# Output blocks 2 and 3 computed ahead at the end of the attention, with the partial sums of blocks 0 and 1 parked in DRAM

## The chip, the cores and the metric

The kernel runs on one core of a Trainium2 chip. The metric is the device time of one execution in microseconds. Engines are named as the profile names them: PE is TensorE, DVE is VectorE, ACT is ScalarE, POOL is GpSimd, SP is SyncE, whose queue here issues most of the DMA transfers. PSUM is the memory that matmuls add into; the kernel uses it in banks of 128 x 512 float32.

## What is computed

Two layers of a decoder on 1024 tokens of width 1024: a retention layer, then a differential attention with 16 heads. The change lies where the second layer's attention ends and its output projection begins. Cut to that part, the reference is:

```python
def diff_attn_mixer(h, w_in, w_out, ...):
    proj = h @ w_in                       # q, k, v and the gate g
    ...                                   # two softmaxes a head, their difference times v
    out = lax.map(block, (qb, starts))    # (heads, tokens, 128)
    out = rmsnorm(out, subln_g, eps=GN_EPS) * (1.0 - lambda_init)
    y = out.transpose(0, 2, 1, 3).reshape(B, S, D_INNER)
    gated = jax.nn.silu(g.astype(jnp.float32)) * y
    return gated.astype(w_out.dtype) @ w_out

x = x + rmsnorm(y, post_norm_g[i])
```

The product `gated @ w_out` is 1024 x 2048 times 2048 x 1024.

## The kernel before

**Numbers.** A float32 factor is split into a rounded high part and the rest (`gh`/`gl` or `wh`/`wl`), and a product takes three matmuls: high by high, high by low, low by high. ACT casts the high part, DVE or POOL subtracts it to get the low one.

**Tiles of the output projection.** The tokens are 8 blocks of 128, the output columns two halves of 512, the inner dimension 16 tiles of 128, one for each head. One block and half fills one PSUM bank and takes 16 x 3 matmuls of 128 x 512. `out_mm` issues them for a run of tiles; `gated8` loads eight tiles of gated attention from DRAM and splits them, in three buffers for each part.

**The attention** (`attention_layer`) runs heads and row blocks in the order `ORDER`, a step being one row block of a head: scores, softmax, transposes of the probabilities (`attn_t`), and after two row blocks the product with the values and a sum of squares. The softmax is on DVE and ACT, so PE would wait for it. Between these steps the kernel therefore pulls matmuls from `filler_gen`: the projections of later heads, and at last the output projection of token blocks 0 and 1, as far as it can go, that is inner tiles 0 to 11 of the first half. A clock of estimated PE time decides how many are pulled at each place; `late` is what of the filler is left for the last steps. The banks that these two blocks fill (`heads`) stay in use until the block is finished.

**Why it can go no further.** The gated tiles need a scale for each token and head, which `row_scales` makes in three batches of heads: 0 to 7, 8 to 11, 12 to 15. The last batch exists only when the attention has ended.

**The output stage** (`output_stage(1, ...)`) starts there. It runs blocks 2 to 7 in pairs over inner tiles 0 to 11, each in a bank of its own, and loads the weights of the second half of the columns meanwhile (`second_half`, two 512 KB loads a call). Then it finishes blocks 0 to 7 with the last quarter, inner tiles 12 to 15 (`product(..., 3)`, 12 matmuls a block). For that `gated` loads the raw values of the last four heads (`graw`, three buffers), the gate (`sgl`, one buffer) and the scales (`rsb`, two), multiplies by the gate on DVE and by the scales on POOL, stores the result for the second half, and splits it into `gh` and `gl`. `first` takes the squares and the scaled copy of a finished bank. The second half of the columns follows, block by block, from values stored in DRAM.

**What sets the order.** PE's instructions stand as the code calls them. On DVE, ACT, POOL and SP a scheduler chooses the order when the program is built, and each engine then works strictly in that order. A tile's buffer is given out again when the tile before it has been used for the last time.

Of the kernel before, what the change touches and what calls it, by code (L numbers as in the profile page):

```python
# [10 lines left out]
F32 = mybir.dt.float32  # L11
# [8 lines left out]
P = 128  # L20
# [3 lines left out]
TB = T // P  # L24
# [3 lines left out]
DH = 16  # L28
NE = 16
# [8 lines left out]
GOB = 1  # L38
ORDER = (6, 2, 3, 7, 4, 0, 1, 5)
LATE = 12  # L40
RATE = 40.4
BATCHES = ((0, 8), (8, 12), (12, 16))
LAMBDA_INIT = 0.8 - 0.6 * math.exp(-0.3)
# [7 lines left out]
class _Trunk:  # L51
# [59 lines left out]
        nc.vector.tensor_sub(gl, raw, _f32(gh))  # L111
        return gh, gl

    def out_mm(self, ps, g, slots, kt0, n, g0=0):
        nc = self.nc
        gh, gl = g
        for k in range(n):
            kt = kt0 + k
            w = slice((kt % 2) * 512, (kt % 2) * 512 + 512)
            wh, wl = (x[:, w] for x in slots[kt // 2])  # L120
            k += g0
            nc.tensor.matmul(ps, gh[:, k, :], wh, start=(kt == 0), stop=False)  # L122
            nc.tensor.matmul(ps, gh[:, k, :], wl, start=False, stop=False)  # L123
            nc.tensor.matmul(ps, gl[:, k, :], wh, start=False, stop=(kt == NE - 1))  # L124
            yield 0.65

    def norm_rows(self, pool, xt, gbc):
# [322 lines left out]
    def output_stage(self, layer, slots, nextR, prologue, head):  # L450
        nc, io = self.nc, self.io
        with ExitStack() as es:
# [4 lines left out]
            fp = self.pool(es, "fsb")  # L457
# [20 lines left out]
            def product(ps, hf, tb, kq):  # L478
                if WIDE[layer][hf] > kq:
                    if kq % 2 == 0:  # L480
                        for _ in self.out_mm(ps, self.gated8(layer, ((tb, kq * 4, 8),)), slots[hf], kq * 4, 8):
                            pass
                    return
                for _ in self.out_mm(ps, gated(tb, kq, hf), slots[hf], kq * 4, 4):
                    pass
# [6 lines left out]
            def second_half(t0):  # L492
                for t in (t0, t0 + 1):
                    self.load_out(layer, slots, 1, t, fp.tile([P, D], F32, tag="x", name="w_raw", bufs=2))

            def first(tb, ps):
                if not acc:
                    acc["y"] = fp.tile([P, TB, 512], F32, name="yacc")
                    acc["ss"] = fp.tile([P, TB, 2], F32, name="ssq")
                    acc["postg"] = fp.tile([P, D], F32, name="postg")  # L500
                    nc.sync.dma_start(acc["postg"], io["post_g"][layer:layer + 1, :].broadcast_to([P, D]))
                    if layer == 0:
                        acc["preg"] = fp.tile([P, D], F32, name="preg")
                        nc.sync.dma_start(acc["preg"], io["pre_g"][1:2, :].broadcast_to([P, D]))
                junk = fp.tile([P, D], F32, tag="x", name="junk", bufs=2)
                nc.scalar.activation(junk[:, 0:512], ps, AF.Square, accum_out=acc["ss"][:, tb, 0:1])
                nc.vector.tensor_mul(acc["y"][:, tb, :], ps, acc["postg"][:, 0:512])
                if layer == 0 and tb % 2 == 0:
                    second_half(tb)

            if layer == 0:
                lead = 2
                g = [self.gated8(0, ((tb, 8, 8),)) for tb in range(lead)]
                for tb in range(lead):
                    for _ in self.out_mm(head[tb], g[tb], slots[0], 8, 8):
                        pass
                    first(tb, head[tb])
            else:
                for t in range(6, 8):
                    self.load_out(1, slots, 0, t)  # L520
                for tb in range(2, TB, 2):
                    two = (tb, tb + 1)
                    g = [self.gated8(1, ((t, 0, 8),)) for t in two]
                    head += [bank() for t in two]
                    for t in two:
                        for _ in self.out_mm(head[t], g[t - tb], slots[0], 0, 8):
                            pass
                    g8 = self.gated8(1, tuple((t, 8, 4) for t in two))
                    for t in two:
                        for _ in self.out_mm(head[t], g8, slots[0], 8, 4, 4 * (t - tb)):  # L530
                            pass
                    second_half(tb - 2)
                second_half(TB - 2)
                for tb in range(TB):
                    product(head[tb], 0, tb, 3)
                    first(tb, head[tb])
                lead = TB
            for tb in range(lead, TB):
                ps = bank()
# [5 lines left out]
            for tb in range(TB):  # L545
# [3 lines left out]
                ps = bank()  # L549
# [25 lines left out]
    def attention_layer(self, HR, QR, pmm, ws0, slots):  # L575
        nc, io = self.nc, self.io
        with ExitStack() as es:
# [8 lines left out]
            wk = self.pool(es, "l1w")  # L586
# [31 lines left out]
            early = []  # L618
            heads = []

            def g_proj(h):
# [4 lines left out]
                for hf in range(2):  # L626
# [6 lines left out]
                    if h >= LATE:  # L633
                        nc.sync.dma_start(self.sgd[4 * hf:4 * hf + 4, :, h - LATE, :].rearrange("t p q -> p t q"), sg.rearrange("p (t q) -> p t q", t=4))
                    out.append(sg)
# [31 lines left out]
            def filler_gen():  # L667
                for h in range(1, DH):
                    yield from qk_proj(h)
                    if h % 2 == 0:  # L670
                        yield from v_proj(h // 2)
                    if h < LATE:
                        yield from g_proj(h)
                for h in range(LATE, DH):
                    yield from g_proj(h)
                for t in range(4, 6):
                    self.load_out(1, slots, 0, t)
                g = self.gated8(1, ((0, 8, 4), (1, 8, 4)))
                for tb in range(2):
                    ps = pmm.tile([P, 512], F32, tag="mm", name="ps_mm", bufs=2)  # L680
                    heads.append(ps)
                    yield from self.out_mm(ps, early[tb], slots[0], 0, 8)
                for tb in range(2):
                    yield from self.out_mm(heads[tb], g, slots[0], 8, 4, 4 * tb)

            filler = filler_gen()
            clk = {"pe": 0.0, "fill": 0.0}
# [177 lines left out]

            seq = [(h, i) for h in range(DH) for i in ORDER]
            total = 15 * 20.8 + 7 * 20.8 + (LATE - 1) * 10.4
            late = (DH - LATE) * 10.4 + 15.6
            load_bias(0)
            for _ in self.l1_qk(HR, QR, pmm, 0, ((0, 1), (1, 1)), ws0):  # L870
                pass
# [12 lines left out]
            for s, (h, i) in enumerate(seq):  # L884
                nxt = seq[s + 1] if s + 1 < len(seq) else None
# [60 lines left out]
    def run(self):  # L946
        nc, ctx = self.nc, self.ctx
# [14 lines left out]
        self.g0 = self.dr.tile([TB, P, NE, P], F32, name="g0")  # L962
        self.g1r = [self.dr.tile([TB, P, h1 - h0, P], F32, name="g1r%d" % h0) for h0, h1 in BATCHES]
        self.g1f = [self.dr.tile([TB, P, 8, P], F32, name="g1f%d" % k) for k in range(2)]
        self.x1d = self.dr.tile([T, D], F32, name="x1d")
        self.sgd = self.dr.tile([TB, P, DH - LATE, P], F32, name="sgd")
        self.ssd = [self.dr.tile([TB, h1 - h0, P], F32, name="ssd%d" % h0) for h0, h1 in BATCHES]
# [6 lines left out]
        pmm = self.pool(ctx, "pmm", PSUM)  # L974
# [16 lines left out]
        with ExitStack() as manual:  # L991
# [7 lines left out]
            early = [a(i) for i in (0, 1, 2, 3, 4, 12, 13, 14)] + [b(i) for i in range(8)]  # L999
# [3 lines left out]
            heads = self.attention_layer(RB, RA, pmm, ws0, pairs)  # L1003
# [78 lines left out]
```

## Time and profile before

| | us |
|---|---|
| median of 3 runs | 2182.5 (2181.49 to 2183.46) |
| the profiled execution, its own time | 2179.38 |
| its span | 2177.6 |
| PE busy in the span | 2132.8 (98%) |
| DVE, ACT, POOL busy | 1283.4, 851.6, 429.3 |

The span is what the trace covers, from the first instruction to the last. The attention of the second layer ends at about 2003 us, the last quarter of the first half runs from about 2055 to 2079, and the second half of the columns takes the rest. "Busy" of PE counts matmuls whose ends are modelled and which overlap, so the pace of PE is read from their starts. A row of a timeline gives start, duration, engine, line and operation, and in brackets how long the engine stood idle before it and what ended that.

### The profile page before, as it was taken

What the parts mean: (1) busy time and instruction counts of PE and PEld (TensorE: products, weight loads), DVE (VectorE), ACT (ScalarE), POOL (GpSimd) and SP (SyncE); (2) the same over time, 40 slices, a digit from 0 to 9 for tenths busy, and PEclk for the clock granted to TensorE, in tenths of its full rate; (3) what the DMA queues carried; (4) which work ended last, traced back from release to release, by engine and by line L of the source; (5) the groups of instructions that cost most, each with busy time, mean ns of one, the idle gap of its engine ahead of it and who ended that gap; (6) DMA issues with size and microseconds to landing.
All of it is one profiled execution on the core that took longest, in us unless ns stands there. A gap on an engine that the chain in (4) does not pass through costs nothing.

```text
span 2177.6 us, 31046 instructions
## 1 busy us (share of the span) xinstructions
PE 2132.8 (98%) x11861; PEld 1790.8 (82%) x11861; DVE 1283.4 (59%) x3155; ACT 851.6 (39%) x1638; POOL 429.3 (20%) x246
## 2 busy tenths in 40 slices
PE   8999999999999999999999999999999999999998
PEld 7888988898897888787888888888787878877776
DVE  6254344334437438646777666767766777776644
ACT  4121221122123333335455555554545555554321
POOL 2332501511512000121111111111133111211300
PEclk9999999999999999999999999999999999999999
DMA  4112112111213545311111111111244113334743
GB/s 167 62 39 68 57 39 73 47 54 54 64 57 99 179 155 174 113 48 42 49 37 42 49 40 42 39 38 43 84 135 136 47 38 95 112 104 146 257 150 134
DMA packets 98916, 185.48 MB, mean 85 GB/s; under 512 B 8848, under 2 KB 51024, under 8 KB 98640
## 3 DMA queue, kind: packets, MB, share of 16 engines
q1 hardware_dynamic: 63824, 166.50, 23.6%
q10 hardware_dynamic: 34944, 17.01, 2.6%
q8 instruction: 93, 1.52, 0.3%
q14 instruction: 55, 0.45, 0.1%
HBM read 147.67 MB, written 38.95 MB: 86 GB/s over the span
## 4 chain that ended last, share of the span: by engine, by line
PE 92%; DVE 3%; issue 1%; ACT 1%; DMA 1%; POOL 0%; ACTq 0%; DVEq 0%; POOLq 0%
PE ps_mm L158 6%; PE ps_mm L157 6%; PE ps_mm L159 5%; PE ps_mm L215 5%; PE ps_mm L122 5%; PE ps_mm L124 5%; PE ps_mm L123 5%; PE ps_mm L217 5%; PE ps_mm L216 5%; PE ps_t L809 3%; PE ps_ret L396 3%; PE ps_s L752 3%; PE ps_mm L650 3%; PE ps_mm L651 3%; PE ps_mm L652 3%; PE ps_mm L167 3%
## 5 line engine op out<-in xcount | busy, mean ns | idle before, releaser
L83 POOL TENSOR_TENSOR w_l<-w_raw,w_h 128x1024 fp32r<-128x1024 f32 x112 | 271.2, 2427 | 1168.8 <-ACT w_h L82 1165.3
L785 ACT ACTIVATE e<-ps_s,nm 128x896 f32<-128x896 f32 (+7 forms) x256 | 189.8, 742 | 103.4 <-DVE nm L783 93.8
L215 PE MATMUL ps_mm<-RB,w_h 128*128 128x512 f32 x512 | 209.4, 409 | 0.4 <-ACT RB L150 0.4
L157 PE MATMUL ps_mm<-RA,w_h 128*128 128x512 f32 x512 | 203.9, 398 | 1.2 <-DVE sg L426 1.1
L158 PE MATMUL ps_mm<-RA,w_h 128*128 128x512 f32 x512 | 204.6, 400 | 0.0
L216 PE MATMUL ps_mm<-RB,w_h 128*128 128x512 f32 x512 | 201.9, 394 | 1.0 <-DVE RB L151 1.0
L217 PE MATMUL ps_mm<-RB,w_l 128*128 128x512 f32 x512 | 202.5, 395 | 0.0
L159 PE MATMUL ps_mm<-RA,w_l 128*128 128x512 f32 x512 | 201.9, 395 | 0.0
L812 ACT CAST ath<-ps_t 128x512 fp32r<-128x512 f32 (+1 forms) x192 | 91.9, 479 | 227.0 <-PE ps_t L809 217.5
L780 DVE TENSOR_REDUCE mx<-ps_s 128x1 f32<-128x640 f32 (+2 forms) x192 | 119.5, 622 | 78.7 <-PE ps_s L755 74.4
L82 ACT CAST w_h<-w_raw 128x1024 fp32r<-128x1024 f32 x112 | 117.6, 1050 | 123.2 <-PE ps_mm L158 39.0
L650 PE MATMUL ps_mm<-w_h,RB 128*128 128x256 f32 x512 | 147.4, 288 | 0.0
L169 PE MATMUL ps_mm<-w_h,RA 128*128 128x256 f32 x512 | 146.1, 286 | 0.0
L167 PE MATMUL ps_mm<-w_h,RA 128*128 128x256 f32 x512 | 145.3, 285 | 0.5 <-ACT RA L150 0.5
L168 PE MATMUL ps_mm<-w_l,RA 128*128 128x256 f32 x512 | 145.2, 285 | 0.1
L111 DVE TENSOR_TENSOR g_l<-w_raw,g_h 128x1024 fp32r<-128x1024 f32 x60 | 82.7, 1378 | 105.7 <-ACT g_h L110 105.6
L651 PE MATMUL ps_mm<-w_l,RB 128*128 128x256 f32 x512 | 143.6, 280 | 0.0
L652 PE MATMUL ps_mm<-w_h,RB 128*128 128x256 f32 x512 | 143.6, 280 | 0.0
L110 ACT CAST g_h<-w_raw 128x1024 fp32r<-128x1024 f32 x60 | 63.0, 1051 | 172.2 <-PE ps_mm L123 126.4
L157 PEld LDWEIGHTS ps_mm<-RA,w_h 128*128 128x128 f32 x512 | 96.1, 188 | 24.5 <-DVE sg L426 1.6
L217 PEld LDWEIGHTS ps_mm<-RB,w_l 128*128 128x128 f32 x512 | 96.1, 188 | 23.7
L159 PEld LDWEIGHTS ps_mm<-RA,w_l 128*128 128x128 f32 x512 | 96.2, 188 | 22.3
(211 smaller groups left out, 5392.7 us busy)
## 6 DMA issues: line engine op xcount, KB each, us to landing
w_raw<-in_wn SPq DMA_DIRECT2D x64, 512.0 KB
w_raw<-in_wv SPq DMA_DIRECT2D x32, 512.0 KB
w_raw<-in_wo SPq DMA_DIRECT2D x32, 512.0 KB
w_raw<-g SPq DMA_DIRECT2D x32, 512.0 KB
w_raw<-g1f SPq DMA_DIRECT2D x24, 512.0 KB
xt<-in_x SPq DMA_DIRECT2D x16, 512.0 KB
w_raw<-in_wg SPq DMA_DIRECT2D x16, 512.0 KB
g<-go ACTq DMA_DIRECT2D x32, 256.0 KB
```

The source lines that it names most:

```text
L83: nc.gpsimd.tensor_sub(l, raw, _f32(h))
L157: nc.tensor.matmul(ps, wh[:, k], region[:, kt, cols], start=(kt == 0), stop=False)
L158: nc.tensor.matmul(ps, wh[:, k], region[:, 8 + kt, cols], start=False, stop=False)
L159: nc.tensor.matmul(ps, wl[:, k], region[:, kt, cols], start=False, stop=(kt == KT - 1))
L167: nc.tensor.matmul(ps, region[:, kt, cols], wh[:, k], start=(kt == 0), stop=False)
L215: nc.tensor.matmul(ps, wh[:, k], HR[:, kt, tok], start=(kt == 0), stop=False)
L216: nc.tensor.matmul(ps, wh[:, k], HR[:, 8 + kt, tok], start=False, stop=False)
L217: nc.tensor.matmul(ps, wl[:, k], HR[:, kt, tok], start=False, stop=(kt == KT - 1))
L650: nc.tensor.matmul(ps[:, t, :], HR[:, kt, cols], wh[:, k], start=(kt == 0), stop=False)
L651: nc.tensor.matmul(ps[:, t, :], HR[:, kt, cols], wl[:, k], start=False, stop=False)
L652: nc.tensor.matmul(ps[:, t, :], HR[:, 8 + kt, cols], wh[:, k], start=False, stop=(kt == KT - 1))
L785: nc.scalar.activation(e[:, 0:n], S[:, 0:n], AF.Exp, bias=nm, accum_out=(s0 if m == 0 else s1))
```

## The change

Blocks 2 and 3 join the filler. `AHEAD_TB = 4` says how many blocks go ahead. When blocks 0 and 1 have run inner tiles 0 to 11, ACT copies their banks to SBUF and stores them to a DRAM tensor `part`; the two banks then take blocks 2 and 3, which stay in them as blocks 0 and 1 did before. In the output stage blocks 4 to 7 run ahead of the last quarter, where 2 to 7 did. Blocks 0 and 1 then take a fresh bank for the last quarter, which starts a sum of its own, and `first` adds the parked partial sum on DVE. The tile into which it is loaded has the tag `graw`, that of the raw values of the last four heads. `late` rises from 41.6 + 15.6 to 41.6 + 31.2.

```diff
@@ out_mm
-    def out_mm(self, ps, g, slots, kt0, n, g0=0):
+    def out_mm(self, ps, g, slots, kt0, n, g0=0, k_first=0, k_last=NE - 1):
...
-            nc.tensor.matmul(ps, gh[:, k, :], wh, start=(kt == 0), stop=False)
+            nc.tensor.matmul(ps, gh[:, k, :], wh, start=(kt == k_first), stop=False)
             nc.tensor.matmul(ps, gh[:, k, :], wl, start=False, stop=False)
-            nc.tensor.matmul(ps, gl[:, k, :], wh, start=False, stop=(kt == NE - 1))
+            nc.tensor.matmul(ps, gl[:, k, :], wh, start=False, stop=(kt == k_last))
@@ output_stage
-            def first(tb, ps):
+            def first(tb, ps, part=None):
...
+                if part is not None:
+                    nc.vector.tensor_add(part, ps, part)
+                    ps = part
                 junk = fp.tile([P, D], F32, tag="x", name="junk", bufs=2)
...
-                for tb in range(2, TB, 2):
+                for tb in range(AHEAD_TB, TB, 2):
...
-                    second_half(tb - 2)
-                second_half(TB - 2)
+                    second_half(tb - AHEAD_TB)
+                for t in range(TB - AHEAD_TB, TB, 2):
+                    second_half(t)
                 for tb in range(TB):
-                    product(head[tb], 0, tb, 3)
-                    first(tb, head[tb])
+                    if tb < AHEAD_TB - 2:
+                        part = fp.tile([P, 512], F32, tag="graw", name="part", bufs=3)
+                        nc.sync.dma_start(part, self.part[tb])
+                        ps = bank()
+                        for _ in self.out_mm(ps, gated(tb, 3, 0), slots[0], 12, 4, k_first=12):
+                            pass
+                        first(tb, ps, part)
+                    else:
+                        ps = head[tb - AHEAD_TB + 2]
+                        product(ps, 0, tb, 3)
+                        first(tb, ps)
@@ filler_gen
-                for tb in range(2):
-                    ps = pmm.tile([P, 512], F32, tag="mm", name="ps_mm", bufs=2)
-                    heads.append(ps)
-                    yield from self.out_mm(ps, early[tb], slots[0], 0, 8)
-                for tb in range(2):
-                    yield from self.out_mm(heads[tb], g, slots[0], 8, 4, 4 * tb)
+                for t0 in range(0, AHEAD_TB, 2):
+                    last = 11 if t0 + 2 < AHEAD_TB else NE - 1
+                    pss, nxt = [], []
+                    for t in range(2):
+                        pss.append(pmm.tile([P, 512], F32, tag="mm", name="ps_mm", bufs=2))
+                        yield from self.out_mm(pss[t], early[t0 + t], slots[0], 0, 8, k_last=last)
+                        if last == 11:
+                            early.append(self.gated8(1, ((t0 + 2 + t, 0, 8),)))
+                    for t in range(2):
+                        yield from self.out_mm(pss[t], g, slots[0], 8, 4, 4 * t, k_last=last)
+                        if last == 11:
+                            part = wk.tile([P, 512], F32, tag="sg", name="part", bufs=3)
+                            nc.scalar.copy(part, pss[t])
+                            nc.scalar.dma_start(self.part[t0 + t], part)
+                        else:
+                            heads.append(pss[t])
+                    if last == 11:
+                        g = self.gated8(1, ((t0 + 2, 8, 4), (t0 + 3, 8, 4)))
...
-            late = (DH - LATE) * 10.4 + 15.6
+            late = (DH - LATE) * 10.4 + 7.8 * AHEAD_TB
```

How the order moves, at three places. Line numbers of the change are one to some thirty higher for the same statement. First PE at the seam between attention and output stage; `ps_o` holds the last values and, from L845, their sums of squares, and L857 transposes the sums for the last scales. Before:

```order
L824 MATMUL ps_o<-atl,RA 128x128
L825 MATMUL ps_o<-ath,RA 128x128
L845 MATMUL ps_o<-sqh,ones 128x256
L846 MATMUL ps_o<-sql,ones 128x256
L857 MATMUL ps_t<-ident,s0all 32x128
L122 MATMUL ps_mm<-RA,g_h 128x512
```

The same place in the change, where these rows follow a first triple of the same kind, which stands behind the last value product:

```order
L123 MATMUL ps_mm<-RB,g_h 128x512
L124 MATMUL ps_mm<-RB,g_h 128x512
L125 MATMUL ps_mm<-RB,g_l 128x512
L871 MATMUL ps_o<-sqh,ones 128x256
L872 MATMUL ps_o<-sql,ones 128x256
L883 MATMUL ps_t<-ident,s0all 32x128
```

Six output matmuls stand between the last values and their sum of squares, where none stood. In the same way 9 more stand ahead of the scores of the last head's row block 3 (12 for 3), 21 for 15 between the scores and the transposes of its row block 0, and 9 for none ahead of the last value product. In all 144 output matmuls stand before L883, and 72 before L857.

Second, SP's queue behind the seam. `graw_19808`, `graw_19840` and `graw_19868` are the raw values of blocks 0, 1 and 2 before; `graw_19818`, `graw_19854` and `graw_19883` those of the change. Before:

```order
L462 DMA graw_19808<-g1r12_82 128x512
L464 DMA sgl_19810<-sgd_86 128x512
L501 DMA postg_19835<-in_post_g 128x1024
L462 DMA graw_19840<-g1r12_82 128x512
L462 DMA graw_19868<-g1r12_82 128x512
```

The change at the same place:

```order
L542 DMA part_19815<-part_85 128x512
L463 DMA graw_19818<-g1r12_82 128x512
L465 DMA sgl_19820<-sgd_87 128x512
L502 DMA postg_19845<-in_post_g 128x1024
L542 DMA part_19851<-part_85 128x512
```

And ten places later in the same queue:

```order
L470 DMA g1f1_84<-graw_19818 128x512
L92 DMA w_raw_19807<-in_wo1 128x1024
L467 DMA rsb_19887<-rsd12_93 128x512
L107 DMA w_raw_20084<-g1f1_84 128x1024
L107 DMA w_raw_20139<-g1f0_83 128x1024
L463 DMA graw_19854<-g1r12_82 128x512
L92 DMA w_raw_19811<-in_wo1 128x1024
L465 DMA sgl_19885<-sgd_87 128x512
L470 DMA g1f1_84<-graw_19854 128x512
L467 DMA rsb_19915<-rsd12_93 128x512
L463 DMA graw_19883<-g1r12_82 128x512
```

The loads of blocks 1 and 2 stood beside that of block 0; now each stands behind the store of the block before it.

Third, DVE where it makes the low halves of blocks 0 and 1. Before:

```order
L475 TENSOR_TENSOR gl_19818<-graw_19808,gh_19817 128x512
L111 TENSOR_TENSOR g_l_19702<-w_raw_19699,g_h_19701 128x1024
L475 TENSOR_TENSOR gl_19850<-graw_19840,gh_19849 128x512
L94 TENSOR_TENSOR RA_77<-w_raw_19800,RA_77 128x1024
L111 TENSOR_TENSOR g_l_19708<-w_raw_19705,g_h_19707 128x1024
L467 TENSOR_TENSOR graw_19896<-graw_19896,sgl_19898 128x512
```

The change; `g_l_20087` belongs to tiles 8 to 15 of block 0 in the second half of the columns, loaded from what block 0's store wrote:

```order
L476 TENSOR_TENSOR gl_19828<-graw_19818,gh_19827 128x512
L95 TENSOR_TENSOR RA_77<-w_raw_19807,RA_77 128x1024
L112 TENSOR_TENSOR g_l_20087<-w_raw_20084,g_h_20086 128x1024
L468 TENSOR_TENSOR graw_19854<-graw_19854,sgl_19856 128x512
L476 TENSOR_TENSOR gl_19864<-graw_19854,gh_19863 128x512
L112 TENSOR_TENSOR g_l_20142<-w_raw_20139,g_h_20141 128x1024
L507 TENSOR_TENSOR part_19815<-ps_mm_19817,part_19815 128x512
L468 TENSOR_TENSOR graw_19883<-graw_19883,sgl_19885 128x512
L511 TENSOR_TENSOR yacc_19843<-part_19815,postg_19845 128x512
```

The multiplication of block 1 by its gate came before block 0's low half; it now stands behind it, and behind a subtraction of the second half.

## Rows read from the trace of the kernel before

**Rows 1.** Windows: stretch, length; busy us and instructions by engine; clock, DMA share, GB/s

```profile
1950.00:2000.00 50.00, 46.58 (x246) 36.94 (x247) 39.93 (x94) 26.36 (x54) 5.50 (x2) 1.00 0.36 112
2000.00:2050.00 50.00, 47.96 (x212) 38.54 (x211) 27.69 (x37) 17.92 (x20) 17.42 (x8) 1.00 0.78 265
```

**Rows 2.** Waits of PE, 1900 to 2100 us: us in total, times, longest

```profile
PE ps_o L824 <- DVE atl L813: 2.3, 1, 2.3
PE ps_mm L124 <- DVE gl L475: 2.0, 3, 1.3
PE ps_t L809 <- DVE atl L813: 1.8, 2, 1.2
PE ps_o L845 <- DVE go L839: 1.5, 1, 1.5
PE ps_t L809 <- DVE nm L783: 1.0, 1, 1.0
PE ps_s L752 <- ACT e L785: 0.9, 1, 0.9
PE ps_o L823 <- DVE ssr L848: 0.6, 1, 0.6
PE ps_mm L122 <- DVE rsr L860: 0.6, 1, 0.6
```

**Rows 3.** Timeline of PE: seam, first output matmul behind it, first of the last quarter

```profile
2003.33 0.27 PE L857 MATMUL ps_t<-ident,s0all 128*32 128x128 f32 x1
2004.19 0.51 PE L122 MATMUL ps_mm<-RA,g_h 128*128 128x512 f32 x1 [0.59 <-DVE rsr L860]
...
2054.70 0.39 PE L122 MATMUL ps_mm<-RB,gh 128*128 128x512 f32 x1
```

**Rows 4.** Windows behind the wait of 2.3 us that ended at 1927.95

```profile
1927.00:1929.00 2.00, 1.05 (x5) 1.05 (x6) 1.51 (x5) 0.42 (x1) 0.00 (x0) 0.70 0.51 115
1929.00:1931.00 2.00, 2.00 (x7) 1.61 (x7) 1.36 (x4) 1.17 (x4) 0.00 (x0) 0.50 1.00 395
```

**Rows 5.** Groups by line, 2004 to 2080: count, busy us, mean ns, idle before

```profile
L111 DVE TENSOR_TENSOR g_l<-w_raw,g_h 128x1024 fp32r<-128x1024 f32 x9 | 13.4, 1491 | 9.5 <-ACT g_h L110 9.5
L475 DVE TENSOR_TENSOR gl<-graw,gh 128x512 fp32r<-128x512 f32 x8 | 7.4, 919 | 1.2 <-ACT gh L474 1.2
L467 DVE TENSOR_TENSOR graw<-graw,sgl 128x512 f32<-128x512 f32 x8 | 5.5, 688 | 11.4 <-DMA sgl<-sgd 7.6 <-issue 3.7
...
L468 POOL TENSOR_TENSOR graw<-graw,rsb 128x512 f32<-128x512 f32 x8 | 14.4, 1801 | 25.2 <-DVE graw L467 17.5 <-DMA graw<-g1r 3.3 <-DMA rsb<-rsd 2.4
...
L474 ACT CAST gh<-graw 128x512 fp32r<-128x512 f32 x8 | 4.9, 618 | 13.4 <-POOL graw L468 13.4
```

**Rows 6.** Timeline: block 0's low half on DVE, and the store of its values

```profile
2033.13 1.78 DVE L475 TENSOR_TENSOR gl<-graw,gh 128x512 fp32r<-128x512 f32 x1
...
2033.61 0.42 SPq L469 DMA_DIRECT2D g1f<-graw  x1
```

**Rows 7.** Timeline: two loads of `sgl` and the multiplications that waited for them

```profile
2065.50 0.32 SPq L464 DMA_DIRECT2D sgl<-sgd  x1
...
2068.88 0.32 SPq L464 DMA_DIRECT2D sgl<-sgd  x1
...
2068.16 0.69 DVE L467 TENSOR_TENSOR graw<-graw,sgl 128x512 f32<-128x512 f32 x1
...
2073.35 0.69 DVE L467 TENSOR_TENSOR graw<-graw,sgl 128x512 f32<-128x512 f32 x1 [3.30 <-DMA sgl<-sgd]
```

**Rows 8.** Timeline: store of the last scales on ACT's queue, first load of them

```profile
2021.00 0.33 ACTq L864 DMA_DIRECT2D rsd<-rsr  x1
...
2025.92 0.79 SPq L466 DMA_DIRECT2D rsb<-rsd  x2
```

**Rows 9.** Timeline: a 512 KB load of stored values, and the cast that waited for it

```profile
2053.36 0.39 SPq L106 DMA_DIRECT2D w_raw<-g1f  x1
...
2058.31 1.05 ACT L110 CAST g_h<-w_raw 128x1024 fp32r<-128x1024 f32 x1 [3.54 <-DMA w_raw<-g1f]
```

More of the change, by code (lines that the diff above doesn't have):

```diff
@@ L40 @@
 LATE = 12
+AHEAD_TB = 4
 RATE = 40.4
@@ L525, in output_stage @@
                     for t in two:
-                        for _ in self.out_mm(head[t], g[t - tb], slots[0], 0, 8):
+                        for _ in self.out_mm(head[t - AHEAD_TB + 2], g[t - tb], slots[0], 0, 8):
                             pass
@@ L529, in output_stage @@
                     for t in two:
-                        for _ in self.out_mm(head[t], g8, slots[0], 8, 4, 4 * (t - tb)):
+                        for _ in self.out_mm(head[t - AHEAD_TB + 2], g8, slots[0], 8, 4, 4 * (t - tb)):
                             pass
-                    second_half(tb - 2)
-                second_half(TB - 2)
+                    second_half(tb - AHEAD_TB)
+                for t in range(TB - AHEAD_TB, TB, 2):
+                    second_half(t)
                 for tb in range(TB):
-                    product(head[tb], 0, tb, 3)
-                    first(tb, head[tb])
+                    if tb < AHEAD_TB - 2:
[9 more added lines that the diff above has]
+                        first(tb, ps)
                 lead = TB
@@ L964, in run @@
         self.g1f = [self.dr.tile([TB, P, 8, P], F32, name="g1f%d" % k) for k in range(2)]
+        self.part = self.dr.tile([AHEAD_TB - 2, P, 512], F32, name="part")
         self.x1d = self.dr.tile([T, D], F32, name="x1d")
```

## The prediction, made before the change was run

> **What bounds the kernel now.** I read the table of windows first, then TensorE's (PE's) waits, then single instructions around the seam between the attention and the last output projection. The windows [rows 1] say where time can be had: PE is busy 46.6 of 50 us in the last stretch of the attention and 48.0 of 50 in the stretch after it. So PE is the bound and only its waits can be won. The waits of PE from 1900 to 2100 us [rows 2] are eight kinds. Seven of them, 2.3 + 1.8 + 1.5 + 1.0 + 0.9 + 0.6 + 0.6 = 8.7 us, lie at the end of the attention, 0.6 of it (L122 on `rsr`) at the seam itself, which nothing moves. The eighth, 2.0 us in three waits, lies where blocks are finished with the last quarter of the inner dimension: PE waits there for `gl`, the low half of the last four heads' gated values. That chain is the other thing to watch: it can only begin when the attention has ended.
>
> **The pace of PE.** The scales of the last heads are transposed at 2003.33, the first matmul of blocks 2 to 7 starts at 2004.19, the first one of the last quarter at 2054.70 [rows 3]. Between the two lie 6 blocks x 36 matmuls = 216, so one takes 50.51 / 216 = 0.234 us, a block's twelve tiles (36 matmuls) 8.4 us, and its last quarter (12 matmuls) 2.8 us.
>
> **What the change moves.** 72 matmuls, 16.8 us, go from behind the seam to before it. No product is saved, since blocks 0 and 1 still run their last quarter, in a bank of their own. So a gain can only be PE's idle time, and the sum has two halves.
>
> **Half one: the end of the attention.** The order shows which waits get new matmuls ahead. The scores of the last head's row block 3 get 9 matmuls more (0.9 us, L752 on `e`), the transposes of its row block 0 have 21 filler matmuls behind their scores where 15 stood, 1.4 us more (1.0 us, L809 on `nm`), the last value sums `ps_o` get 9 (0.6 us, L823 on `ssr`), the last sum of squares gets 6, that is 1.4 of its 1.5 us. Together 0.9 + 1.0 + 0.6 + 1.4 = 3.9 us. Ahead of the 2.3 us wait and the two of 1.8 stands the same number of fillers as before, so I leave them. Bounds: 0, if the new casts and subtractions on ScalarE (ACT) and VectorE (DVE) push other waits out; 9.7, if all 8.1 us go and with them the clock loss of the 2.3 us wait. That loss is 1.6 us: after this wait the granted clock stood at 0.70 and 0.50 for 2 us each [rows 4], so 0.6 + 1.0 us were lost. The copies of the two partial sums, their stores (on ACT's queue) and their loads are costed at nothing: DVE has 10 us idle in the 50 and ACT 24 [rows 1]. If that cover were gone, two copies of a size that takes about 0.6 us (as the cast in [rows 5]) would cost 1.2.
>
> **Half two: behind the seam.** PE now needs the first last quarter after 4 blocks, not 6: at 2054.7 - 16.8 = 2037.9 on the old clock (times from here on count so, the seam held at 2003.3). Block 0's `gl` was done at 2033.13 + 1.78 = 2034.9 [rows 6], so block 0 is in time with 3 us to spare. Block 1 is not. The old kernel loads `graw` of blocks 0, 1 and 2 at once, into three buffers. In the new one `part` shares the tag: the two partial sums take two of the three, from right after the seam, and hold them until blocks 0 and 1 are through PE and their squares and products are taken. In the new order the load of block 1's `graw` stands behind block 0's store, and it waits for block 0's `gl`, since it gets the only buffer left; block 2's waits for block 1's in turn.
>
> Block 1, low end: load issued at 2034.9, 2.66 to the multiplication by `sgl` (the quiet pair, 2065.50 to 2068.16, [rows 7]), then 0.69 + 1.80 + 0.62 + 0.92 for the two multiplications, the cast and the subtraction [rows 5]: ready at 2041.6, due at 2037.9 + 2.8 = 2040.7, so 0.9 us of waiting. High end: on DVE block 1's multiplication now stands behind the subtraction for the second half's first tiles, whose load needs block 0's stored result. The store goes out at 2033.61 [rows 6]; a store and the load that depends on it are 4.9 us apart (2021.00 to 2025.92, [rows 8]), a 512 KB load lands 4.95 later (2053.36 to 2058.31, [rows 9]); 1.05 for the cast [rows 9], 1.49 for the subtraction [rows 5] and the 4.03 above follow: 2050.1, 9.4 us of waiting. I take 5.0, the middle: the order puts it on the long path, but the long path's transfers were priced where the weights load too.
>
> Block 2: from the end of block 1's multiplication on GpSimd (POOL), its store must land (2.66 if it takes as long as the quiet load, an estimate; or 4.9), the load (2.66 or 4.47) and 4.03 of engines follow, against 1.54 (cast and subtraction) and 2.8 of product that PE has meanwhile: 9.35 - 4.34 = 5.0, or 13.4 - 4.34 = 9.1. I take 5.0, since the weights are in by then.
>
> Blocks 3 to 7 go at the pace of `sgl`, which has one buffer: load, multiply, next load. Two rows give load to multiplication as 2.66 and 4.47 [rows 7], + 0.69 + 0.03 to the next issue, + 0.32 for the issue of a `graw` load that the new order sets in between: 3.7 or 5.5 us against 2.8. I take the mean, 4.6: 5 x 1.8 = 9.0 (ends 4.5 and 13.5). The old kernel has the same loop, but ran it under 50 us of other products.
>
> The Trainium skill, "DMA: Bandwidth & Descriptors", section "Anatomy of one DMA", fits a transfer as about 2.0 us and its bytes at 436 GB/s, for transfers that GpSimd issues; 256 KB would take 2.6 us. The row of 2.66 agrees, the one of 4.47 does not; by the page alone the loop would be 3.7 us, the term 4.5 instead of 9.0.
>
> Waits behind the seam are thus 5.0 + 5.0 + 9.0 = 19.0 us, against 2.0 before. After the last the second half begins at a lowered clock: 1.6 us, as in [rows 4].
>
> **Sum.** -3.9 - 2.0 + 19.0 + 1.6 = +14.7 us. The profiled execution took 2179.38, 2177.6 of it span, so it would take 2194.1; the median of the three runs, 2182.5, lies 3.1 above it, and I give the time against that: 2197.2.
>
> **Rivals.** (1) *The clock stays low through the stage.* PE would work 2.8 us and wait 2, eight times over. [rows 4] show the half level after one wait; against it, the three waits of 2.0 us in all [rows 2] left no such mark. At half clock a block takes 5.6 us, more than the loop's 4.6, and PE sets the pace: 7 blocks x 1.0 more, 2204. The Trainium skill, "TensorE: Matmul & The Clock Gate", section "HAM oscillation", speaks against the change here: where every burst waits for a transfer, each begins cold. That is this rival.
>
> (2) *Quiet transfers.* The stage at its low ends, 0.9 + 5.0 + 4.5 = 10.4, no clock loss: -3.9 - 2.0 + 10.4 = +4.5, 2187. For it: 1.5 MB of loads leave the stretch that moved 265 GB/s [rows 1], and 0.5 MB of partial sums come. Against it: the same 4 MB of weights must come in 33.6 us instead of 50.
>
> (3) *Faster.* The fillers clear the attention's end: all 9.7 us, because spread work also pulls DVE's long subtractions apart. It decides as soon as the stage waits less than 9.7 + 2.0 = 11.7 us; at the low ends, 10.4, the time is 2181.2, and under 7.3 it would be faster by more than 0.2%, some 2175 at 5. Against it: the longest wait has the same fillers ahead.
>
> (4) *It does not do what it says*: the moved matmuls run behind the seam after all, 2182. The order speaks against it; all 72 stand before the last transposes.
>
> **How the numbers follow.** Forecast 0.62; low clock 0.17; quiet transfers 0.12; faster 0.05; no effect 0.04. The low clock and the forecast's upper ends reach 2205, quiet transfers 2187; together with the tails some 2 in 10 stay outside. A measurement tells about 0.2%, 4.4 us, from no change, so 2186.9 and above counts as slower: faster 0.05, same 0.08 (no effect, and a third of the quiet case), slower 0.87.
>
> **What would show it.** In the new profile: the waits of L752, L809 on `nm`, L823 and L845 gone, the 2.3 us wait still there; the last transposes of the scales about 13 us later; PE waiting for `gh` or `gl` before nearly each of blocks 1 to 7, some 19 us; block 1's `graw` load issued after block 0's `gl`. I would be wrong if block 1's load went out beside block 0's, if the loop over `sgl` took 3 us, or if the seam came less than 9 us later.

## The result, and the profile after

The changed kernel takes 2196.6 us (median of 4 runs, 2195.2 to 2198.2), the kernel before took 2182.0 beside it (4 runs, 2181.2 to 2183.5). The ratio is 1.0067, with a 95% interval of 1.0055 to 1.0079: slower by 14.6 us. The forecast was 2197.2.

The trace splits into four stretches at starts of TensorE (PE) instructions that both kernels have. The first is the transposes of the second batch of scales (heads 8 to 11), the next those of the last batch, the seam of [rows 3]. In the timeline of before, PE:

```profile
1751.39 0.28 PE L857 MATMUL ps_t<-ident,s0all 128*32 128x128 f32 x1 [1.40 <-DVE atl L813]
```

and in that of after:

```profile
1752.52 0.29 PE L883 MATMUL ps_t<-ident,s0all 128*32 128x128 f32 x1 [1.40 <-DVE atl L839]
...
2016.76 0.27 PE L883 MATMUL ps_t<-ident,s0all 128*32 128x128 f32 x1
...
2094.91 0.39 PE L123 MATMUL ps_mm<-RB,g_h 128*128 128x512 f32 x1
```

The last row is the first matmul of the second half of the columns; the first one of a last quarter starts at 2051.34.

| stretch | before, us | after, us | difference |
|---|---|---|---|
| start to the second scales | 1751.39 | 1752.52 | +1.1 (nothing was changed there) |
| attention, second to last scales | 251.94 | 264.24 | +12.3 = 16.8 moved - 4.5 |
| cover, last scales to first last quarter | 51.37 | 34.57 | -16.8 |
| stage, the last quarters of 8 blocks | 25.24 | 43.58 | +18.3 |
| second half of the columns | 97.64 | 97.80 | +0.2 |
| span | 2177.6 | 2192.7 | +15.1 |

So the attention's end did gain, and the stage behind the seam lost four times as much. PE's waits in the changed kernel from 1900 to 2110 us (what it waited for, us in total, times, longest; they answer to [rows 2]):

```profile
PE ps_mm L123 <- ACT gh L475: 10.2, 5, 5.2
PE ps_mm L125 <- DVE gl L476: 2.4, 2, 1.4
PE ps_o L850 <- DVE atl L839: 2.3, 1, 2.3
PE ps_t L835 <- DVE e L817: 2.1, 4, 0.8
...
PE ps_t L835 <- DVE atl L839: 0.3, 1, 0.3
```

The first two are the stage's, 12.6 us where 2.0 stood; the wait of 0.6 us for `rsr` at the seam is there as before. In the timeline of after, PE, the first two are seven rows, of which these are four (start, duration, and in brackets the wait); the other three waits are 1.34, 0.90 and 1.20 us, ahead of blocks 3, 5 and 6:

```profile
2059.47 0.79 PE L123 MATMUL ps_mm<-RB,gh 128*128 128x512 f32 x1 [5.17 <-ACT gh L475]
2061.68 0.80 PE L125 MATMUL ps_mm<-RB,gl 128*128 128x512 f32 x1 [0.99 <-DVE gl L476]
2067.47 0.50 PE L123 MATMUL ps_mm<-RB,gh 128*128 128x512 f32 x1 [1.57 <-ACT gh L475]
...
2088.14 0.50 PE L125 MATMUL ps_mm<-RB,gl 128*128 128x512 f32 x1 [1.43 <-DVE gl L476]
```

From block to block the stage takes 8.14, 8.00, 6.21, 3.55, 4.22, 4.52, 5.75 and 3.19 us, where pure products take 2.80: 21.2 us over. The waits are 12.6 of that. Of the other 8.6, some 5 us are matmuls at a lowered clock: 22 of them start 0.43 us apart instead of 0.234, which is 4.3 us, and the starts around the wait of 0.99 are slow too. The other 3.5 or so lie at the full clock, as pauses of up to 0.3 us beside the waits and ahead of the low products that the list does not name: at 2077.23, 2077.57 and 2077.96, with the granted clock at 1.00, three matmuls start 0.34 and 0.39 us apart. The windows of after (length, busy times of PE, its weight loads, VectorE (DVE), ScalarE (ACT) and GpSimd (POOL), granted clock, share and GB/s of the DMA engines) show where the clock was low:

```profile
2060.00:2065.00 5.00, 4.01 (x10) 2.64 (x9) 4.02 (x5) 1.09 (x3) 1.08 (x1) 0.50 0.71 231
2065.00:2070.00 5.00, 3.43 (x11) 2.12 (x10) 2.71 (x5) 1.24 (x3) 1.60 (x1) 0.84 0.91 305
2070.00:2075.00 5.00, 3.57 (x10) 2.08 (x10) 2.54 (x4) 1.19 (x3) 1.27 (x1) 0.79 0.80 251
2075.00:2080.00 5.00, 4.87 (x21) 3.32 (x20) 2.08 (x4) 1.31 (x3) 1.83 (x2) 1.00 0.71 235
...
2090.00:2092.00 2.00, 2.00 (x6) 1.59 (x5) 0.61 (x1) 0.00 (x0) 0.00 (x0) 0.50 0.38 139
```

Why block 1 was late is read from the timeline of after, all engines, in order of time:

```profile
2045.96 0.32 SPq L470 DMA_DIRECT2D g1f<-graw  x1
...
2048.46 0.80 SPq L107 DMA_DIRECT2D w_raw<-g1f  x2
2049.30 0.43 SPq L463 DMA_DIRECT2D graw<-g1r  x1
...
2054.46 1.04 ACT L111 CAST g_h<-w_raw 128x1024 fp32r<-128x1024 f32 x1 [3.14 <-DMA w_raw<-g1f]
2055.54 1.22 DVE L112 TENSOR_TENSOR g_l<-w_raw,g_h 128x1024 fp32r<-128x1024 f32 x1 [2.96 <-ACT g_h L111]
2056.68 0.68 DVE L468 TENSOR_TENSOR graw<-graw,sgl 128x512 f32<-128x512 f32 x1
2057.50 1.27 POOL L469 TENSOR_TENSOR graw<-graw,rsb 128x512 f32<-128x512 f32 x1 [7.38 <-DVE graw L468]
2058.80 0.62 ACT L475 CAST gh<-graw 128x512 fp32r<-128x512 f32 x1 [0.19 <-POOL graw L469]
```

Block 0's product is stored (L470), the second half's load that needs it follows (L107), and only then block 1's raw values are loaded (L463), 4.8 us before PE could take their product. Their multiplication by the gate (L468) stands on DVE behind the subtraction of those second-half tiles (L112), which waits for its load. PE starts block 1 at 2059.47, when the cast has ended.

Block 2 got the same buffer next. Timeline of after, DVE and SP:

```profile
2059.45 2.17 DVE L476 TENSOR_TENSOR gl<-graw,gh 128x512 fp32r<-128x512 f32 x1 [2.08 <-ACT gh L475]
...
2061.65 0.32 SPq L463 DMA_DIRECT2D graw<-g1r  x1
...
2064.34 0.69 DVE L468 TENSOR_TENSOR graw<-graw,sgl 128x512 f32<-128x512 f32 x1 [0.98 <-DVE part L507]
```

Its raw values are loaded as block 1's `gl` ends (2061.62), and its cast ends at 2067.42, just ahead of PE's start at 2067.47.

### The profile page after: what moved, and what is told of

Its sections match the earlier page's. It is cut to its first block, busy times and chain, and to the rows that moved or that the text cites. A ratio compares the mean times of both kernels' runs of the same rounds, so it can differ in the third digit from the quotient of the medians.

```text
span 2192.7 us, 31043 instructions
## 1 busy us (share of the span) xinstructions
PE 2138.4 (98%) x11861; PEld 1792.9 (82%) x11861; DVE 1281.4 (58%) x3157; ACT 853.0 (39%) x1640; POOL 425.2 (19%) x246
## 4 chain that ended last, share of the span: by engine, by line
PE 89%; DVE 4%; DMA 3%; ACT 2%; issue 1%; POOL 0%; SPq 0%; DVEq 0%; ACTq 0%; POOLq 0%
PE ps_mm L159 6%; PE ps_mm L158 5%; PE ps_mm L160 5%; PE ps_mm L216 5%; PE ps_mm L218 5%; PE ps_mm L217 5%; PE ps_mm L123 4%; PE ps_mm L124 4%; PE ps_mm L125 4%; PE ps_t L835 3%; PE ps_ret L397 3%; PE ps_s L778 3%; PE ps_mm L664 3%; PE ps_mm L665 3%; PE ps_mm L666 3%; PE ps_mm L168 3%
## 5 line engine op out<-in xcount | busy, mean ns | idle before, releaser
L112 DVE TENSOR_TENSOR g_l<-w_raw,g_h 128x1024 fp32r<-128x1024 f32 x60 | 83.2, 1387 | 103.2 <-ACT g_h L111 103.2
```

## What the experiments measured

In all traces the attention is taken from the second to the last scales, since the runs differ by up to 3.7 us ahead of that, where no kernel was changed. Ratios are against the kernel before on the same chip (2182.8 us for the first four, 2184.2 for the last four).

| kernel | median, us | ratio (95%) | attention | cover | stage |
|---|---|---|---|---|---|
| before | 2182.0 | | 251.94 | 51.37 | 25.24 |
| after | 2196.6 | 1.0067 (1.0055 to 1.0079) | 264.24 | 34.57 | 43.58 |
| own_part | 2184.7 | 1.0008 (0.9999 to 1.0018) | 264.38 | 34.57 | 32.86 |
| two_gates | 2190.5 | 1.0031 (1.0021 to 1.0041) | 264.46 | 34.57 | 37.07 |
| own_part_two_gates | 2184.2 | 1.0004 (0.9994 to 1.0014) | 264.31 | 34.57 | 30.36 |
| before_part_tiles | 2192.6 | 1.0042 (1.0027 to 1.0057) | 251.75 | 52.92 | 33.36 |
| warm_waits | 2203.0 | 1.0088 (1.0071 to 1.0104) | 264.43 | 34.57 | 49.53 |
| before_two_gates | 2181.2 | 0.9987 (0.9978 to 0.9995) | 252.13 | 51.37 | 23.05 |
| cover_back | 2174.7 | 0.9960 (0.9947 to 0.9972) | 264.02 | 51.37 | 22.40 |
| cover_back_late | 2171.6 | 0.9946 (0.9933 to 0.9958) | 260.51 | 52.90 | 22.40 |

**own_part: the partial sums in tiles of their own.**

```diff
-                        part = fp.tile([P, 512], F32, tag="graw", name="part", bufs=3)
+                        part = fp.tile([P, D], F32, tag="yo", name="part", bufs=2)[:, 0:512]
```

> The change, but the two partial sums are loaded into tiles of their own (the tag yo, which nobody uses before the second half), so that graw keeps its three buffers. Theory A, buffers: the waits ahead of blocks 1 and 2 (5.3 and 5.2 us over a block's 2.8 in the changed kernel) come from the shared tag; block 1's load then goes out before block 0's gl is done, and the stage of 43.6 us gets 6 to 10 us shorter: 2187 to 2191. Theory B, cover: after the last scales the loads, products and casts take as long as they do, 34.6 us of other products are too few to hide them, and what blocks 1 and 2 no longer wait, blocks 3 to 5 do: 2194 to 2197.

The time fell by 12 us, more than theory A said. Its timeline, SP's queue, has the raw values of blocks 0 to 2 issued by 2029.5, where the changed kernel issued block 1's at 2049.30:

```profile
2020.53 0.42 SPq L463 DMA_DIRECT2D graw<-g1r  x1
...
2028.24 0.32 SPq L542 DMA_DIRECT2D part<-part  x1
2028.61 0.91 SPq L463 DMA_DIRECT2D graw<-g1r  x2
```

Blocks 0 and 1 then take 2.80 us each: of the stage's 18.3 us, tiles of their own take away 10.7. Theory B keeps a part: block 2 takes 8.25, and PE waits 3.64 us for its `gl`, so the stage is still 7.6 us longer than before. DVE shows that this wait is one of order too:

```profile
2059.34 1.22 DVE L112 TENSOR_TENSOR g_l<-w_raw,g_h 128x1024 fp32r<-128x1024 f32 x1 [1.70 <-ACT g_h L111]
...
2061.09 0.68 DVE L476 TENSOR_TENSOR gl<-graw,gh 128x512 fp32r<-128x512 f32 x1
```

Block 2's high half was cast by 2054.70, but on DVE its low half (L476) stands behind a subtraction of the second half (L112), which waited for its own cast, and behind block 0's add.

**two_gates: a second buffer for the gate, the sharing kept.**

```diff
-                    sg = fp.tile([P, 4, P], F32, tag="sgl", name="sgl")
+                    sg = fp.tile([P, D], F32, tag="yo", name="sgl", bufs=2)[:, 0:512].rearrange("p (t q) -> p t q", t=4)
```

> The change, but the gate tile sgl has two buffers (in the tag yo) where it had one; the partial sums still share graw. Theory A, the loop over sgl sets the pace of blocks 3 to 7 (10.6 us over 2.8 a block in the changed kernel), blocks 1 and 2 keep their waits: 6 to 8 us less, 2189 to 2191. If another step of the chain sets that pace (POOL's product, the store, the two buffers of gl), the time stays within 2 us of 2196.6.

As theory A said. Blocks 0 and 1 keep 6.98 and 8.07 us; blocks 2 to 7 take 5.50, 3.80, 2.80, 3.43, 3.70 and 2.80, that is 5.2 us over 2.8 each instead of 10.6. Of these 5.2, block 2 has 2.7, without a listed wait: its matmuls ran at half clock (0.50 from 2066 to 2070).

**own_part_two_gates: both.**

```diff
+                    if tb % 2 == 0:
                         sg = fp.tile([P, 4, P], F32, tag="sgl", name="sgl")
+                    else:
+                        sg = fp.tile([P, D], F32, tag="yo", name="sgl", bufs=2)[:, 0:512].rearrange("p (t q) -> p t q", t=4)
...
-                        part = fp.tile([P, 512], F32, tag="graw", name="part", bufs=3)
+                        if tb == 0:
+                            parts = fp.tile([P, 2, 512], F32, tag="yo", name="part", bufs=2)
+                        part = parts[:, tb, :]
```

> The change with both: a tile of its own for the two partial sums, and a second buffer for the gate of the odd blocks. Theory A: nothing is left in short supply, the stage falls from 43.6 us to 26 or 30, and the kernel to 2180 to 2185; under 2177 only if the stage came down to the 22.4 of pure products. Theory B, cover: the blocks come out of a chain that is late by 16.8 us whatever the buffers, 4 us or more each: 2187 to 2192.

Within theory A's range, at its slow end: the stage is 30.4 us, and the ratio cannot be told from own_part's, since the intervals overlap. With all three buffers to spare the stage is still 5 us longer than before. That rest is put down to the shorter cover, which cover_back tests.

**before_part_tiles: the sharing alone, nothing moved.**

```diff
+                    part = None
+                    if tb < 2:
+                        part = fp.tile([P, 512], F32, tag="graw", name="part", bufs=3)
+                        nc.sync.dma_start(part, io["x"][tb * P:tb * P + P, 0:512])
                     product(head[tb], 0, tb, 3)
+                    if part is not None:
+                        nc.vector.tensor_add(part, head[tb], part)
                     first(tb, head[tb])
```

> The kernel before, with no product moved, and only the two tiles of the partial sums added: blocks 0 and 1 each load 256 KB (rows of x) into a tile with the tag graw and add it to the bank on DVE, with a result that nothing uses. So graw is in as short supply as in the change, but 51 us of products still lie between seam and last quarter. If the sharing alone costs its 10 us wherever it stands: 2190 to 2194. If it costs only because the cover was taken away as well (block 1 is ready 44.8 us after the seam in the changed kernel, and is due here 54.2 us after it): 2182 to 2185.

It was the first case. Blocks 0 and 1 are in time, as worked out beforehand, but the wait comes two blocks later. The loads of raw values on SP's queue and DVE's rows show why. SP:

```profile
2039.79 0.32 SPq L462 DMA_DIRECT2D graw<-g1r  x1
...
2051.85 0.32 SPq L462 DMA_DIRECT2D graw<-g1r  x1
...
2066.89 2.36 SPq L462 DMA_DIRECT2D graw<-g1r  x3
```

DVE and PE of the same kernel:

```profile
2065.04 1.23 DVE L111 TENSOR_TENSOR g_l<-w_raw,g_h 128x1024 fp32r<-128x1024 f32 x1 [4.36 <-ACT g_h L110]
2066.18 0.68 DVE L541 TENSOR_TENSOR part<-ps_mm,part 128x512 f32<-128x512 f32 x1
2066.78 0.68 DVE L475 TENSOR_TENSOR gl<-graw,gh 128x512 fp32r<-128x512 f32 x1
```

```profile
2067.52 0.50 PE L124 MATMUL ps_mm<-RB,gl 128*128 128x512 f32 x1 [2.28 <-DVE gl L475]
2073.30 0.80 PE L122 MATMUL ps_mm<-RB,gh 128*128 128x512 f32 x1 [3.17 <-ACT gh L474]
```

The one buffer that is left carries blocks 1 and 2, 12 us apart. Then nothing can be loaded until block 0's sum is added, which ends at 2066.86; the next loads go out at 2066.89. Block 0 was through PE at 2061.81, but on DVE the add stands behind a subtraction for the second half, which waited 4.36 us for its cast. So the 3.17 us ahead of block 3 are the buffer's, while the 2.28 us in block 2 come from DVE's order: its `gl` (L475) stands behind both. A tile that is loaded early and used late keeps its buffer all that time, whatever cover stands ahead.

With own_part this makes a square of four stages:

| stage, us | tiles of their own, or none | `graw` shared |
|---|---|---|
| 51 to 53 us of cover | 25.2 (before) | 33.4 |
| 34.6 us of cover | 32.9 | 43.6 (after) |

Read so, the sharing costs 8.1 or 10.7, the shorter cover 7.6 or 10.2, and of the stage's 18.3 us, 15.7 are the two alone and 2.6 what they add to each other. Two limits: each cell is one trace with the order on DVE that came with it, and in the upper row the step from 25.2 to 33.4 also holds the two loads and two adds themselves, since the kernel before has none. A kernel before with these two tiles in a tag of their own was not run.

**before_two_gates: the second gate buffer in the kernel before** (the edit of two_gates).

> The kernel before, with a second buffer for the gate and nothing else. Its stage takes 25.2 us against 22.4 of pure products. If the loop over sgl is what it waits for: 1 to 2.8 us less, a ratio of 0.9987 to 0.9996; if something else is, the ratio is 1.000 within its interval.

The stage falls from 25.24 to 23.05 and the ratio is 0.9987: the loop over `sgl` is what the kernel before waited for as well, for 2.2 of the stage's 2.8 us.

**warm_waits: zero products in PE's waits.**

```diff
+WARM = (0, 20, 20, 13, 3, 6, 7, 12)
...
+            def warm(ps, n, fresh):
+                for k in range(n):
+                    nc.tensor.matmul(ps, zero, slots[0][0][0][:, 0:512], start=(fresh and k == 0), stop=(fresh and k == n - 1))
...
+                        warm(ps, WARM[tb], False)
```

> The change, with 81 matmuls of a zero tile ahead of the last quarters of blocks 1 to 7 (20, 20, 13, 3, 6, 7, 12), 0.23 us each at full clock, which add nothing and wait for nothing, so that PE works where it waited. If the lowered clock in the stage costs what its slowed matmuls lose (8.6 us of the 21.2 that the blocks take over 2.8 each): 2188 to 2191. My reading is that the chain of loads, products and casts sets the pace, and PE's slow matmuls hide in it but for the last ones: 2194 to 2197, with the granted clock near 1 through the stage.

Neither. The granted clock is 1.00 from 2051 to 2080 and the first five blocks take 7.46, 7.47, 5.83, 3.50 and 5.73 us, 30.0 together as in the changed kernel (30.1). But 20 zero products and a block are 20 x 0.234 + 2.8 = 7.48 us, so in the first four the added products set the pace and not the chain. And the order on the other engines, which is chosen when the kernel is built, came out otherwise: block 5 waited 3.70 us for its `gl` and took 11.14. How much of the slow matmuls lay on the path (some 5 us, not the 8.6 that the expectation names) stays open for this run; the changed kernel's own trace says something of it below.

**cover_back: the cover given back.**

```diff
+                side = [bank() for _ in range(2)]
+                for tb in range(2):
+                    for _ in self.out_mm(side[tb], self.gated8(1, ((tb, 0, 8),)), slots[1], 0, 8):
+                        pass
+                g8 = self.gated8(1, ((0, 8, 4), (1, 8, 4)))
+                for tb in range(2):
+                    for _ in self.out_mm(side[tb], g8, slots[1], 8, 4, 4 * tb):
+                        pass
-                for tb in range(TB):
+                for tb in (2, 3, 4, 5, 6, 7, 0, 1):
...
-            for tb in range(TB):
+            for tb in range(TB) if layer == 0 else (2, 3, 0, 1, 4, 5, 6, 7):
...
+                if layer == 1 and tb < 2:
+                    ps = side[tb]
+                    if tb == 0:
+                        g8 = self.gated8(1, ((0, 12, 4), (1, 12, 4)))
+                    for _ in self.out_mm(ps, g8, slots[1], 12, 4, 4 * tb):
+                        pass
```

These edits stand on top of own_part_two_gates.

> The change with the partial sums in a tile of their own and a second gate buffer, and the cover given back: the two banks that are free run inner tiles 0 to 11 of blocks 0 and 1 of the second half of the columns (72 matmuls) ahead of the last quarters, which then come in the order 2 to 7, 0, 1, and the second half in the order 2, 3, 0, 1, 4 to 7. If the loss of the change is buffers and cover alone, the stage comes down to 22 to 24 us and the 3.4 us that the attention's end gained are kept: a ratio of 0.9965 to 0.998 (2175 to 2178). If the stage still takes 30 us as with own buffers alone, 1.000 or more.

Faster than both kernels, and a little faster than I expected. The stage takes 22.40 us, eight blocks of 2.80, and PE waits for no `gh` or `gl` any more. Its waits from 1900 to 2110, beside 0.6 for `rsr` at the seam:

```profile
PE ps_o L870 <- DVE atl L859: 2.3, 1, 2.3
PE ps_t L855 <- DVE atl L859: 1.8, 1, 1.8
PE ps_t L855 <- DVE e L837: 1.7, 3, 0.7
```

So buffers and cover together account for the whole loss. The edit also puts blocks 0 and 1, with their parked sums, last in the stage; no run separates that from the cover. In the trace 4.7 us are gained in the attention (251.94 + 16.8 - 264.02) and 2.8 in the stage, 7.5 in all; the ratio says 8.7, with 6.1 to 11.6 as its interval.

**cover_back_late: more filler left for the last steps.**

```diff
-            late = (DH - LATE) * 10.4 + 7.8 * AHEAD_TB
+            late = (DH - LATE) * 10.4 + 8.4 * AHEAD_TB
```

> As cover_back, but the pull clock leaves 8.4 us of filler a block for the last steps where it left 7.8, so that more products stand between the last steps of the attention. If the 4.7 us that PE still waits there (2.3 for atl, 2.1 for e, 0.3) and the clock that it loses behind the first can be had by it: 2 to 4 us below cover_back. If the 2.3 us wait has as many products ahead as before: the same as cover_back within 1 us.

3.1 us below cover_back by the medians, the fastest of all; its slowest run (2172.7) lies below cover_back's fastest (2173.3). The 4.7 us of the expectation are the waits of the changed kernel; cover_back's own were 5.8. The waits here from 1900 to 2110:

```profile
PE ps_o L891 <- DVE go L885: 1.1, 1, 1.1
PE ps_mm L123 <- DVE rsr L906: 0.6, 1, 0.6
PE ps_t L855 <- DVE e L837: 0.5, 1, 0.5
PE ps_t L855 <- DVE atl L859: 0.4, 1, 0.4
PE ps_o L870 <- DVE atl L859: 0.2, 1, 0.2
```

The wait of 2.3 us that had stood in every kernel so far is down to 0.2. The attention gains 3.5 us more, 8.2 against before (251.94 + 16.8 - 260.51). The cover is 1.5 us longer, since PE's clock fell behind the seam.

## The prediction, step by step

The time, the sign and the place of the loss were right. Not all of the terms were right for the reason given:

**Half one, forecast -3.9, measured -4.5.** The four waits that were to go did go (L752, L809 on `nm`, L823, L845), and the 2.3 us wait stayed, with the clock loss behind it. Two things were not foreseen: the two waits on `atl` shrank from 1.8 to 0.3, and four new short ones on `e` came, 2.1 in all. They about cancel. The sum of listed waits fell by 3.4 (8.1 to 4.7, without the 0.6 at the seam); the other 1.1 has no row.

**The cover, forecast 34.6 us (33.6 of it products), measured 34.57,** and block 0 in time: right. It starts at 2051.34, and its `gl` was done at 2047.6.

**Block 1, forecast 5.0, measured 5.3 (8.14 - 2.80).** That the middle of two paths came out is luck. The path was the long one, as the order had it: store, second-half load, cast, subtraction, block 1's own chain. For that path the prediction had 9.4, and its steps were 4.1 too dear in all. The store to the dependent load took 2.5 us (2045.96 to 2048.46) where I used 4.9 from [rows 8]; the store went out 29.2 us behind the seam where I had 30.3; PE began without the 0.92 for `gl`, since its first matmuls need only `gh`; POOL's multiplication took 1.27 instead of 1.80 and the subtraction 1.22 instead of 1.49. Against that, the 512 KB load took 6.0 (2048.46 to 2054.46) where I used 4.95 from [rows 9].

**Block 2, forecast 5.0, measured 5.2.** Here the chain held, too: it goes from block to block through the one buffer that is left. From the end of block 1's multiplication on POOL (2058.77) to the end of block 2's `gl` (2067.45 + 0.69) are 9.37 us, forecast 9.35, and the load of the raw values took 2.69, forecast 2.66. The load went out as block 1's `gl` ended, which took 2.17 us; whether the store had landed before that, which the prediction asked for, the trace does not show. Of the 5.2 only 0.99 + 1.57 are listed waits. The rest is for the most part PE at half clock, so a reader of the wait table alone sees half the loss. The slow matmuls cost little here, though: block 2 could not start before its cast had ended at 2067.42, however fast block 1 ran.

**Blocks 3 to 7, forecast 9.0, measured 9.1.** From the start of block 2 to the end of block 7 the stage is 10.6 over 2.8 a block, and 1.5 of that is the clock loss of the last two, which has a term of its own. The size came out, but a second buffer for `sgl` takes away only about half of it. Its last five loads in the changed kernel's timeline, SP:

```profile
2065.06 0.32 SPq L465 DMA_DIRECT2D sgl<-sgd  x1
...
2071.11 0.37 SPq L465 DMA_DIRECT2D sgl<-sgd  x1
2075.45 0.38 SPq L465 DMA_DIRECT2D sgl<-sgd  x1
2079.76 0.38 SPq L465 DMA_DIRECT2D sgl<-sgd  x1
2083.89 0.32 SPq L465 DMA_DIRECT2D sgl<-sgd  x1
```

They are 6.05, 4.34, 4.31 and 4.13 us apart; the forecast was 4.6, between 3.7 and 5.5. The first step was not set by `sgl`: block 3's multiplication (2070.06) waited for its raw values, in the shared tag. The last load made PE's wait of 1.43 us: block 6's `gl` (2087.40) stands on DVE behind block 7's multiplication, which waited 2.32 for `sgl`. In two_gates 5.4 of the 10.6 go, the 1.5 of clock loss at the end among them, and 5.2 stay. An estimate from the Trainium skill's fit of one DMA ("DMA: Bandwidth & Descriptors", section "Anatomy of one DMA"), weighed in the prediction, would have made the loop 3.7, below all four.

**Clock loss, forecast 1.6, measured 1.5.** The eight matmuls from 2089.17 to 2092.58 took 3.41 us instead of 8 x 0.234 = 1.87. Nothing waits after them, so all of it is on the path. It fell in the last two blocks, not at the start of the second half, so the size came out and the place did not.

**Sum.** -4.5 + 18.3 + 0.2 = +14.0, and 1.1 more by which this run was late ahead of the attention's last steps; forecast +14.7.

**The rivals.** (1) The half level lasted from about 2059 to 2065, from 2069 to 2072 and from 2089 to 2092; from 2075 to 2080 the clock was 1.00. The clock did not stay low, but it fell more often than I had it. A block at half clock takes 12 x 0.43 = 5.1 us, not the 5.6 that the rival counts with. The Trainium skill ("TensorE: Matmul & The Clock Gate", section "HAM oscillation") tells of bursts that each begin cold where the wait ahead of a burst is longer than the burst. The trace agrees: only the wait of 5.17 us is longer than a block's 2.8, and only the block behind it began at half clock. Behind the waits of 1.57 and 1.43 us PE began at full clock and the clock fell 1.4 and 1.0 us later; behind those of 1.34, 0.90 and 1.20 it stayed at 1.00. (2) The quiet prices were met between store and load (2.5) and by block 2's load (2.69); the 512 KB load and the loop were dearer. (3) The mechanism was possible: cover_back_late takes 8.2 of the 9.7 us that it names, by other means than moving the products alone. (4) The products did move.

One thing the prediction did not separate. It blamed the shared tag for blocks 1 and 2, and in the square the lost cover weighs about as much (10.2 and 10.7 us in the changed kernel).

## What to carry to other kernels

Work that is moved ahead of a barrier no longer hides the chain behind it: count what the moved work was covering, as well as what it fills. An engine that works in a fixed order passes waits on: twice here, in own_part and before_part_tiles, a low half whose cast was long done stood on DVE behind a subtraction that waited for another cast. A tile that parks a value until late takes a buffer from every tile of its tag for all that time, and 53 us of cover did not pay for that here (33.4 us against 25.2 with nothing moved, the two loads and adds included). When a good move loses, keep it and repair what it took away: the same move with a tile of its own, a second gate buffer and other work as cover made 0.9960 out of 1.0067, and one constant of the filler's pace 0.9946.

## What was not expected of the hardware

The same short waits left different clocks behind them. At the seam PE waits 1.1 to 1.5 us for `go` and 0.6 for `rsr` in several of these kernels. Windows behind it, of before, before_part_tiles and cover_back_late in this order:

```profile
2003.00:2005.00 2.00, 1.41 (x6) 0.90 (x6) 0.94 (x4) 0.00 (x0) 0.00 (x0) 1.00 0.47 102
2005.00:2007.00 2.00, 2.00 (x10) 1.64 (x9) 0.00 (x0) 0.00 (x0) 0.00 (x0) 1.00 0.95 299
```

```profile
2006.00:2008.00 2.00, 1.41 (x7) 0.96 (x8) 0.89 (x3) 0.00 (x0) 0.00 (x0) 1.00 0.56 123
2008.00:2010.00 2.00, 2.00 (x6) 1.60 (x5) 0.00 (x0) 0.00 (x0) 0.00 (x0) 0.50 1.00 317
```

```profile
2014.00:2016.00 2.00, 2.00 (x7) 1.54 (x5) 0.00 (x0) 0.00 (x0) 0.00 (x0) 0.50 0.91 295
```

The clock went on at 1.00 (2.4 GHz) in the first and fell to 0.50 (1.2 GHz) in the other two, and the cover was 1.5 us longer for it (52.92 and 52.90 against 51.37). What decides it, these traces do not show. The stretch ahead of the second scales, where no kernel was changed, also differed by up to 3.7 us between runs (1751.39 to 1755.13), so a sum of a few us is safer made from a mark just ahead of the change than from the span.
